# Loading the weights of a bilinear form as float32 from SyncE instead of casting them to bf16 on the way, and multiplying in four column groups

## The chip, the cores and the metric

One core of one Trainium2 chip (trn2). The metric is device time in microseconds of that core, the median of several executions; lower is better. The time is some 1.8 us above the span of the profile, which runs from the first to the last instruction. "Fast" here means within 1.5% of the fastest run of the same kernel; ratios use fast runs.

## The reference

```python
# x: [32, 256], y: [32, 256], weight: [128, 256, 256], all float32
def reference(x, y, weight):
    return np.einsum('bi,bj,kij->bk', x, y, weight).astype(np.float32)
```

The weights are 33.55 MB and are used once; everything else is small. PE contracts over i (x against the rows of the weights), VectorE multiplies by y and sums over j.

## The kernel before

```python
    x2_sb = consts.tile([B, 2, I], f32)          # x twice, for two row groups
    nc.sync.dma_start(out=x2_sb[:, 0, :], in_=x)
    nc.sync.dma_start(out=x2_sb[:, 1, :], in_=x)
    y_sb = consts.tile([B, J], f32)
    nc.sync.dma_start(out=y_sb, in_=y)
    # ... (identity; four transposes; xT in bf16: row kg*64 + ip holds x[b, 4*ip + ic])
    w_rearr = weight.rearrange("k (ip ic) j -> ip k (ic j)", ic=CHUNK)   # CHUNK = 4: runs of 4 KiB

    for kt in range(NUM_K_TILES):                # 32 tiles of 4 k
        k0 = kt * K_TILE
        wtile = wpool.tile([P, K_HALF, CHUNK * J], bf16)                 # wpool: 4 buffers
        for kg in range(2):
            nc.gpsimd.dma_start(                 # float32 in memory, bf16 in SBUF: a cast on the way
                out=wtile[kg * HALF_P:(kg + 1) * HALF_P, :, :],
                in_=w_rearr[:, k0 + kg:k0 + K_TILE:2, :],
            )
        for ks in range(0, K_HALF, K_SUB):
            # ... (two PSUM tiles)
            for ic in range(CHUNK):
                for kg in range(2):
                    p0 = kg * HALF_P
                    nc.tensor.matmul(            # 64 rows, 32 columns, 256 moving columns
                        out=psums[kg][:B, :].rearrange("b (k j) -> b k j", k=K_SUB),
                        lhsT=xT[p0:p0 + HALF_P, ic, :],
                        rhs=wtile[p0:p0 + HALF_P, ks:ks + K_SUB, ic * J:(ic + 1) * J],
                        start=(ic == 0), stop=(ic == CHUNK - 1),
                    )
            for kg in range(2):
                # ... (per k: tensor_tensor_reduce of psum * y_sb into out_sb[:, k], 32 partitions)
    nc.sync.dma_start(out=out, in_=out_sb)
```

Of the kernel before, what the change touches and what calls it, by code (L numbers as in the profile page):

```python
# [1 line left out]

# [5 lines left out]


@with_exitstack
def kernel(
    ctx: ExitStack,
    tc: tile.TileContext,
    x: bass.AP,
    y: bass.AP,
    weight: bass.AP,
    out: bass.AP,
):
    nc = tc.nc  # L20
    P = 128

    B, I = x.shape
    _, J = y.shape
    K, _, _ = weight.shape
    assert x.shape == (B, I)
    assert y.shape == (B, J)
    assert weight.shape == (K, I, J)
    assert out.shape == (B, K)

    CHUNK = 4
    HALF_P = P // 2
    assert I == HALF_P * CHUNK
    assert K <= P
    assert K % 2 == 0

    K_TILE = 4
    assert K % K_TILE == 0 and K_TILE % 2 == 0
    K_HALF = K_TILE // 2
    NUM_K_TILES = K // K_TILE  # L40
    K_SUB = max(1, min(K_HALF, 256 // J))
    assert K_HALF % K_SUB == 0

    f32 = mybir.dt.float32
    bf16 = mybir.dt.bfloat16

    consts = ctx.enter_context(tc.tile_pool(name="consts", bufs=1))
    wpool = ctx.enter_context(tc.tile_pool(name="wpool", bufs=4))
    psum_pool = ctx.enter_context(tc.tile_pool(name="psum", bufs=4, space=bass.MemoryType.PSUM))
    tmps = ctx.enter_context(tc.tile_pool(name="tmps", bufs=2))  # L50

    x2_sb = consts.tile([B, 2, I], f32)
    nc.sync.dma_start(out=x2_sb[:, 0, :], in_=x)
    nc.sync.dma_start(out=x2_sb[:, 1, :], in_=x)
    x2_flat = x2_sb.rearrange("b two i -> b (two i)")

    y_sb = consts.tile([B, J], f32)
    nc.sync.dma_start(out=y_sb, in_=y)

    identB = consts.tile([B, B], f32)  # L60
    make_identity(nc, identB)

    xT = consts.tile([P, CHUNK, B], bf16)
    for ic in range(CHUNK):
        xt_psum = psum_pool.tile([P, B], f32)
        nc.tensor.transpose(  # L66
            out=xt_psum,
            in_=x2_flat[:, ic::CHUNK],
            identity=identB,
        )  # L70
        nc.vector.tensor_copy(out=xT[:, ic, :], in_=xt_psum)  # L71

    out_sb = consts.tile([B, K], f32)

    w_rearr = weight.rearrange("k (ip ic) j -> ip k (ic j)", ic=CHUNK)

    for kt in range(NUM_K_TILES):
        k0 = kt * K_TILE

        wtile = wpool.tile([P, K_HALF, CHUNK * J], bf16)  # L80
        for kg in range(2):
            nc.gpsimd.dma_start(  # L82
                out=wtile[kg * HALF_P:(kg + 1) * HALF_P, :, :],
                in_=w_rearr[:, k0 + kg:k0 + K_TILE:2, :],
            )

        for ks in range(0, K_HALF, K_SUB):
            psums = []
            for kg in range(2):
                psum = psum_pool.tile([P, K_SUB * J], f32)  # L90
                psums.append(psum)
            for ic in range(CHUNK):
                for kg in range(2):
                    p0 = kg * HALF_P
                    nc.tensor.matmul(  # L95
                        out=psums[kg][:B, :].rearrange(
                            "b (k j) -> b k j", k=K_SUB
                        ),
                        lhsT=xT[p0:p0 + HALF_P, ic, :],
                        rhs=wtile[p0:p0 + HALF_P, ks:ks + K_SUB,  # L100
                                  ic * J:(ic + 1) * J],
                        start=(ic == 0),
                        stop=(ic == CHUNK - 1),
                    )

            for kg in range(2):
                psum_view = psums[kg][:B, :].rearrange(
                    "b (k j) -> b k j", k=K_SUB
                )
                for kk in range(K_SUB):  # L110
                    kdst = k0 + 2 * (ks + kk) + kg
                    tmp = tmps.tile([B, J], f32)
                    nc.vector.tensor_tensor_reduce(  # L113
                        out=tmp,
                        in0=psum_view[:, kk, :],
                        in1=y_sb,
                        scale=1.0,
                        scalar=0.0,
                        op0=mybir.AluOpType.mult,
                        op1=mybir.AluOpType.add,  # L120
                        accum_out=out_sb[:, kdst:kdst + 1],
                    )

    nc.sync.dma_start(out=out, in_=out_sb)


# [1 line left out]
_INS = ['x', 'y', 'weight']  # L128
_OUTS = [((32, 128), 'float32')]


# [23 lines left out]
```

## Time and profile before

| | kernel before |
|---|---|
| time, median of 2 runs | 92.69 us (92.67 to 92.71) |
| span of the profile | 90.9 us |
| weights read, rate in the steady part | 33.55 MB, 420 GB/s (210 GB/s landed as bf16) |
| first and last weight packet | 2.81 and 85.76 us after the span's start |
| from the last weight packet to the end | 5.15 us |
| PE, VectorE, GpSimd busy | 73.9, 49.8, 38.0 us |

The lines themselves are in the prediction below. The table is read from the stream outwards: what comes before its first packet (2.81 us), its length (82.95 us), and what follows its last (5.15 us) sum to the span. The packet times are records of the trace. The view of stretches of time shows engines, clock and rate for ten microseconds in the steady part; its columns are named in the first line of the fence:

```profile
core 0: us, PE busy (x) PEld busy (x) DVE busy (x) POOL busy (x), PEclk, DMA share, GB/s
20.00:30.00 10.00, 8.89 (x62) 5.07 (x60) 5.47 (x30) 4.22 (x8) 1.00 1.12 210
```

The last number is the one to follow through this document. It counts bytes that land; for a cast from float32 to bf16 the bytes read are twice that (33.65 MB read, 16.78 landed, by the page).

### The profile page before, as it was taken

How to read it: one execution, taken by the hardware profiler on the slowest of the kernel's cores; microseconds unless marked ns; L12 is line 12 of the kernel's file. 1: busy time of each engine (PE TensorE's matmuls, PEld its weight loads, DVE VectorE, ACT ScalarE, POOL GpSimd, SP SyncE). 2: the span in 40 equal slices, each digit the busy share in tenths (PEclk: the TensorE clock that was granted, in tenths of full speed). 3: DMA queues.
4: the chain of work that ended last, by engine and by line, in shares of the span. 5: the costliest groups of instructions: out<-in, count | busy, mean ns of one | idle time of the engine just before them, and what ended most of it. 6: DMA issues, size and time to landing. Idle time of an engine off the chain costs nothing.

```text
span 90.9 us, 1569 instructions
## 1 busy us (share of the span) xinstructions
PE 73.9 (81%) x516; PEld 42.3 (47%) x516; DVE 49.8 (55%) x260; POOL 38.0 (42%) x70
## 2 busy tenths in 40 slices
PE   0248989899898989669898989898998989899970
PEld 0216444555454545435554545454555545454530
DVE  0213555676535666664556656666555565566650
POOL 5970555544435543650455554434345555500000
PEclk9999999999999999985555555555555555555555
DMA  0799999999999999999999999999999999999300
GB/s 18 121 190 186 197 208 210 207 211 213 207 208 210 208 210 209 209 209 209 211 208 212 209 209 209 211 208 215 203 210 208 211 208 212 207 210 214 53 0 7
DMA packets 9416, 16.99 MB, mean 187 GB/s; under 512 B 1088, under 2 KB 1216, under 8 KB 9408
## 3 DMA queue, kind: packets, MB, share of 16 engines
q0 software_dynamic: 9216, 16.78, 100.1%
q1 hardware_dynamic: 192, 0.11, 0.5%
q8 instruction: 4, 0.07, 0.3%
q14 instruction: 4, 0.03, 0.1%
HBM read 33.65 MB, written 0.02 MB: 370 GB/s over the span
## 4 chain that ended last, share of the span: by engine, by line
DMA 64%; PE 20%; POOL 6%; issue 6%; DVE 1%; DVEq 0%; POOLq 0%
DMA wtile<-in_weight_dram 64%; PE psum L95 20%; POOL wtile L82 6%; DVE tmp L113 1%; DVE out_sb L113 0%; POOL identB masks.py:199 0%; DVEq L150 0%; POOL identB masks.py:197 0%; POOLq masks.py:199 0%; POOLq L139 0%
## 5 line engine op out<-in xcount | busy, mean ns | idle before, releaser
L95 PE MATMUL psum<-wtile,xT 64*32 64x256 bf16 x512 | 73.2, 405 | 11.1 <-DMA wtile<-in_weight_dram 9.3
L113 DVE CUSTOM_DVE_ANT_0 tmp<-psum,y_sb 32x256 f32<-32x256 f32 x128 | 48.6, 409 | 35.4 <-PE psum L95 35.2
L95 PEld LDWEIGHTS <-xT 64*32 64x32 bf16 x512 | 41.8, 122 | 42.2 <-DMA wtile<-in_weight_dram 23.9
L82 POOL DMA_DIRECT2D wtile<-in_weight_dram x64 | 37.5, 596 | 40.7 <-PE psum L95 40.1
L113 DVE DVE_READ_ACCUMULATOR2_ANT out_sb<- 32x1 f32 x128 | 9.1, 71 | 0.0
L66 PE MATMUL xt_psum<-identB,x_sb 32*128 32x32 f32 x4 | 0.7, 300 | 3.0 <-DMA x_sb<-in_x_dram 3.0
L71 DVE CAST xT<-xt_psum 128x32 bf16<-128x32 f32 x4 | 0.6, 192 | 3.4 <-PE xt_psum L66 3.4
L66 PEld LDWEIGHTS xt_psum<-identB,x_sb 32*128 32x128 f32 x4 | 0.6, 208 | 3.0 <-POOL identB masks.py:199 3.0
masks.py:199 POOL TENSOR_SCALAR_AFFINE_SELECT identB<-identB 32x32 f32<-32x32 f32 x1 | 0.2, 229 | 0.1
masks.py:197 POOL MEMSET identB<- 32x32 f32 x1 | 0.1, 114 | 0.3 <-POOLq L139 0.3
L139 POOL MEMSET const-float32-0.0<- 128x1 f32 x1 | 0.1, 103 | 0.2 <-issue 0.2
L139 POOL MEMSET const-bfloat16-1.0<- 128x1 bf16 x1 | 0.1, 106 | 0.0
L139 POOL MEMSET const-uint8-127<- 128x1 uint8 x1 | 0.1, 106 | 0.0
L139 POOL MEMSET const-float32-1.0<- 128x1 f32 x1 | 0.1, 103 | 0.0
## 6 DMA issues: line engine op xcount, KB each, us to landing
wtile<-in_weight_dram POOLq DMA_DIRECT2D x64, 256.0 KB, 7.2
x_sb<-in_x_dram SPq DMA_DIRECT2D x2, 32.0 KB, 1.7
y_sb<-in_y_dram SPq DMA_DIRECT2D x1, 32.0 KB, 3.2
out_dram<-out_sb SPq DMA_DIRECT2D x1, 16.0 KB, 1.4
```

The costliest lines, as they stand in the source:

```text
L66: nc.tensor.transpose(out=xt_psum, in_=x2_flat[:, ic::CHUNK], identity=identB,)
L71: nc.vector.tensor_copy(out=xT[:, ic, :], in_=xt_psum)
L82: nc.gpsimd.dma_start(out=wtile[kg * HALF_P:(kg + 1) * HALF_P, :, :], in_=w_rearr[:, k0 + kg:k0 + K_TILE:2, :],)
L95: nc.tensor.matmul(out=psums[kg][:B, :].rearrange("b (k j) -> b k j", k=K_SUB), lhsT=xT[p0:p0 + HALF_P, ic, :], rhs=wtile[p0:p0 + HALF_P, ...
L113: nc.vector.tensor_tensor_reduce(out=tmp, in0=psum_view[:, kk, :], in1=y_sb, scale=1.0, scalar=0.0, op0=mybir.AluOpType.mult, op1=mybir.Al ...
L139: nc = _bacc.Bacc("TRN2", target_bir_lowering=False, num_devices=1)
```

## The change

The intent: weight loads issued by SyncE (`q1 hardware_dynamic`) instead of GpSimd (`q0 software_dynamic` on the page before), no cast, float32 products. Float32 products take longer. To pay for them, the four k of a tile go into the four column groups of PE, 32 columns each, so that one PSUM tile holds four results on 128 partitions and one reduction serves four k. The contraction has 128 rows now, two per partition, so a run of memory that goes to one partition is 2 KiB; before, four rows per partition made 4 KiB.

```diff
-    wpool = ctx.enter_context(tc.tile_pool(name="wpool", bufs=4))
+    wpool = ctx.enter_context(tc.tile_pool(name="wpool", bufs=16))
...
+    w_v = weight.rearrange("(t g) (p ic) j -> g p t (ic j)", t=T, ic=IC)     # T = 4, IC = 2: runs of 2 KiB
+    x_sb = consts.tile([B, I], f32)
+    nc.scalar.dma_start(out=x_sb, in_=x)
+    y4 = consts.tile([P, J], f32)
+    for t in range(T):
+        nc.scalar.dma_start(out=y4[t * B:(t + 1) * B, :], in_=y)
... (identity; two transposes; xT stays float32)
+    acc = consts.tile([P, G], f32)
+    for g in range(G):                                                       # G = 32
+        wt = wpool.tile([P, T, IC, J], f32)
+        pieces = [(0, T)] if g < G - 1 else [(0, 2), (2, 3), (3, 4)]
+        for lo, hi in pieces:
+            nc.sync.dma_start(
+                out=wt[:, lo:hi, :, :].rearrange("p t ic j -> p t (ic j)"),
+                in_=w_v[g][:, lo:hi, :],
+            )
+        ps = pso.tile([P, J], f32)
+        for ic in range(IC):
+            for t in range(T):
+                nc.tensor.matmul(
+                    out=ps[t * B:(t + 1) * B, :],
+                    lhsT=xT[:, ic, :],
+                    rhs=wt[:, t, ic, :],
+                    start=(ic == 0), stop=(ic == IC - 1),
+                )
+        tmp = tmps.tile([P, J], f32)
+        nc.vector.tensor_tensor_reduce(
+            out=tmp, in0=ps, in1=y4, scale=1.0, scalar=0.0,
+            op0=mult, op1=add, accum_out=acc[:, g:g + 1],
         )
... (all of the loop of the kernel before goes)
-    nc.sync.dma_start(out=out, in_=out_sb)
+    for t in range(T):
+        eng = nc.sync if t % 2 == 0 else nc.scalar
+        eng.dma_start(out=out[:, t * G:(t + 1) * G], in_=acc[t * B:(t + 1) * B, :])
```

More of the change, by code (lines that the diff above doesn't have):

```diff
@@ L21 @@
     P = 128
+    f32 = mybir.dt.float32
+    mult = mybir.AluOpType.mult
+    add = mybir.AluOpType.add
     B, I = x.shape
@@ L25 @@
     K, _, _ = weight.shape
-    assert x.shape == (B, I)
-    assert y.shape == (B, J)
-    assert weight.shape == (K, I, J)
-    assert out.shape == (B, K)
-    CHUNK = 4
-    HALF_P = P // 2
-    assert I == HALF_P * CHUNK
-    assert K <= P
-    assert K % 2 == 0
-    K_TILE = 4
-    assert K % K_TILE == 0 and K_TILE % 2 == 0
-    K_HALF = K_TILE // 2
-    NUM_K_TILES = K // K_TILE
-    K_SUB = max(1, min(K_HALF, 256 // J))
-    assert K_HALF % K_SUB == 0
-    f32 = mybir.dt.float32
-    bf16 = mybir.dt.bfloat16
+    T = P // B
@@ L47 @@
+    IC = I // P
+    G = K // T
+    assert T * B == P and IC * P == I and G * T == K
     consts = ctx.enter_context(tc.tile_pool(name="consts", bufs=1))
-    wpool = ctx.enter_context(tc.tile_pool(name="wpool", bufs=4))
-    psum_pool = ctx.enter_context(tc.tile_pool(name="psum", bufs=4, space=bass.MemoryType.PSUM))
+    wpool = ctx.enter_context(tc.tile_pool(name="wpool", bufs=16))
+    psx = ctx.enter_context(tc.tile_pool(name="psx", bufs=1, space=bass.MemoryType.PSUM))
+    pso = ctx.enter_context(tc.tile_pool(name="pso", bufs=6, space=bass.MemoryType.PSUM))
@@ L50 @@
     tmps = ctx.enter_context(tc.tile_pool(name="tmps", bufs=2))
-    x2_sb = consts.tile([B, 2, I], f32)
-    nc.sync.dma_start(out=x2_sb[:, 0, :], in_=x)
-    nc.sync.dma_start(out=x2_sb[:, 1, :], in_=x)
-    x2_flat = x2_sb.rearrange("b two i -> b (two i)")
-    y_sb = consts.tile([B, J], f32)
-    nc.sync.dma_start(out=y_sb, in_=y)
-    identB = consts.tile([B, B], f32)
-    make_identity(nc, identB)
-    xT = consts.tile([P, CHUNK, B], bf16)
-    for ic in range(CHUNK):
-        xt_psum = psum_pool.tile([P, B], f32)
-        nc.tensor.transpose(
-            out=xt_psum,
-            in_=x2_flat[:, ic::CHUNK],
-            identity=identB,
-        )
-        nc.vector.tensor_copy(out=xT[:, ic, :], in_=xt_psum)
@@ L73 @@
-    out_sb = consts.tile([B, K], f32)
-    w_rearr = weight.rearrange("k (ip ic) j -> ip k (ic j)", ic=CHUNK)
-    for kt in range(NUM_K_TILES):
-        k0 = kt * K_TILE
-        wtile = wpool.tile([P, K_HALF, CHUNK * J], bf16)
-        for kg in range(2):
-            nc.gpsimd.dma_start(
-                out=wtile[kg * HALF_P:(kg + 1) * HALF_P, :, :],
-                in_=w_rearr[:, k0 + kg:k0 + K_TILE:2, :],
-            )
-        for ks in range(0, K_HALF, K_SUB):
-            psums = []
-            for kg in range(2):
-                psum = psum_pool.tile([P, K_SUB * J], f32)
-                psums.append(psum)
-            for ic in range(CHUNK):
-                for kg in range(2):
-                    p0 = kg * HALF_P
-                    nc.tensor.matmul(
-                        out=psums[kg][:B, :].rearrange(
-                            "b (k j) -> b k j", k=K_SUB
-                        ),
-                        lhsT=xT[p0:p0 + HALF_P, ic, :],
-                        rhs=wtile[p0:p0 + HALF_P, ks:ks + K_SUB,
-                                  ic * J:(ic + 1) * J],
-                        start=(ic == 0),
-                        stop=(ic == CHUNK - 1),
-                    )
-            for kg in range(2):
-                psum_view = psums[kg][:B, :].rearrange(
-                    "b (k j) -> b k j", k=K_SUB
-                )
-                for kk in range(K_SUB):
-                    kdst = k0 + 2 * (ks + kk) + kg
-                    tmp = tmps.tile([B, J], f32)
-                    nc.vector.tensor_tensor_reduce(
-                        out=tmp,
-                        in0=psum_view[:, kk, :],
-                        in1=y_sb,
-                        scale=1.0,
-                        scalar=0.0,
-                        op0=mybir.AluOpType.mult,
-                        op1=mybir.AluOpType.add,
-                        accum_out=out_sb[:, kdst:kdst + 1],
-                    )
@@ L124 @@
-    nc.sync.dma_start(out=out, in_=out_sb)
+    w_v = weight.rearrange("(t g) (p ic) j -> g p t (ic j)", t=T, ic=IC)
[4 more added lines that the diff above has]
+        nc.scalar.dma_start(out=y4[t * B:(t + 1) * B, :], in_=y)
+    ident = consts.tile([B, B], f32)
+    make_identity(nc, ident)
+    xt_ps = psx.tile([P, IC, B], f32)
+    for ic in range(IC):
+        nc.tensor.transpose(out=xt_ps[:, ic, :], in_=x_sb[:, ic::IC], identity=ident)
@@ new lines @@
+    xT = consts.tile([P, IC, B], f32)
+    nc.vector.tensor_copy(out=xT, in_=xt_ps)
+    acc = consts.tile([P, G], f32)
[8 more added lines that the diff above has]
+        ps = pso.tile([P, J], f32)
+        for ic in range(IC):
+            for t in range(T):
[9 more added lines that the diff above has]
+            op0=mult, op1=add, accum_out=acc[:, g:g + 1],
+        )
```

## The prediction

The rate of 27.2 GB/s per engine stands, because two records of the trace give it: 8 KiB took 307 ns and 1 KiB 44 ns, so 7168 bytes more took 263 ns more, 27.25 GB/s. The sum came to 92.7 + 2.5 - 1.8 + 0.5 = 93.9 us. One term in it has lost a part: of the tail's 5.2 to 6 us (+0.5), about 2 us for the last five products are cut. The half clock is read from the lengths of records: where the trace of the kernel before has clock records, products last 269 ns at 1.0 (36.9 to 40.3 us) and 417 ns at 0.5 (from 40.3 us to the end).

> **What bounds the kernel now.** I read the page from the end backwards: the chain of work that ended last, then the row of slices, then the queues, then the groups of instructions.
>
> ```profile
> DMA  0799999999999999999999999999999999999300
> GB/s 18 121 190 186 197 208 210 207 211 213 207 208 210 208 210 209 209 209 209 211 208 212 209 209 209 211 208 215 203 210 208 211 208 212 207 210 214 53 0 7
> ...
> q0 software_dynamic: 9216, 16.78, 100.1%
> ...
> HBM read 33.65 MB, written 0.02 MB: 370 GB/s over the span
> ## 4 chain that ended last, share of the span: by engine, by line
> DMA 64%; PE 20%; POOL 6%; issue 6%; DVE 1%; DVEq 0%; POOLq 0%
> ```
>
> The last line, the chain, is mostly waiting for weights (64%). The DMA row is full from slice 2 to slice 36. GB/s counts what lands: 210, because float32 is cast to bf16 on the way, so about 420 are read (33.65 MB read, 16.78 landed). The queue's packets add up to 100% of the span of 16 engines although the stream doesn't fill the span, so packets overlap a little: the bound is the 16 DMA engines, not the issuing.
>
> ```profile
> L95 PE MATMUL psum<-wtile,xT 64*32 64x256 bf16 x512 | 73.2, 405 | 11.1 <-DMA wtile<-in_weight_dram 9.3
> L113 DVE CUSTOM_DVE_ANT_0 tmp<-psum,y_sb 32x256 f32<-32x256 f32 x128 | 48.6, 409 | 35.4 <-PE psum L95 35.2
> L82 POOL DMA_DIRECT2D wtile<-in_weight_dram x64 | 37.5, 596 | 40.7 <-PE psum L95 40.1
> ...
> wtile<-in_weight_dram POOLq DMA_DIRECT2D x64, 256.0 KB, 7.2
> ```
>
> GpSimd waits 40.1 us for buffers, yet that is harmless: a load lands 7.2 us after issue, and 512 KiB read at 420 GB/s take 1.25 us, so about six loads are always queued. PE at 73.2 us busy looks near its limit, but its records overlap. The timeline of PE at 33 to 35 us shows weight loads in pairs starting at 33.47, 33.66, 33.87, 34.08 and 34.30 us: a pair of products (two row groups, 64 rows each) every 0.21 us, so 16 products of a tile take 8 x 0.21 = 1.7 us plus about 0.4 of latency, of the 2.5 us in which the tile arrives.
>
> The packet records of the trace give the pace. Weight packets (4 KiB read, 2 KiB written) run from 2.8 to 85.8 us after the span's start; in the steady part 512 of them take 5.07 us over 16 engines, 158 ns per packet and engine, 414 GB/s read. After the last packet 5.1 us remain until 90.9: the last products (to 88.0), the last reduction (88.6), and about 2.3 us to write the output. The measured time, 92.69, is 1.8 above the span.
>
> [...]
> - [...]the shortest 8 KiB packet took 307 ns (301 at 27.2 GB/s), the shortest 1 KiB packet of the x load 44 ns (37.6), so a packet costs its bytes over 27.2 GB/s plus about 6.3 ns. For the 4 KiB reads that says 157 ns; 158 was seen.
> - [...]
> - [...]No float32 product other than a transpose is in this trace.
> - [...]The trace shows the half clock most of the way ([...]records of 417 ns) with some 269 ns records between 30 and 43 us. It shows two row groups together; column groups it doesn't show.
>
> **The change part by part.**
>
> 1. *Bytes over the DMA engines.* HBM reads stay at 33.55 MB. The written bytes double to 33.55 MB, but the engines were paced by the reads, so this costs nothing unless the write side adds its own limit. What does change is the size of a run: 2 KiB instead of 4 KiB read per packet, hence 16,384 packets instead of 8,192, each with the 6.3 ns again. A packet: 2048 / 27.2 = 75.3 ns, plus 5 to 6.3 = 80.3 to 81.6 ns (estimate from the records above). Per engine 1,024 packets: 82.2 to 83.6 us, and 34 completion writes of 9 to 22 ns, 0.3 to 0.7 us. Sum about 83.4, against 512 x 158 = 80.9 before: **+2.5 us**. If queued packets overlap so well that the fixed part vanishes, it is 77 to 80.
>
> 2. *Start.* The first weight load leaves SyncE first thing (about 0.75 us, where the x load is now) instead of GpSimd at 1.29, and x, y go on ScalarE. The x packets started 1.0 us after their issue, so the weights start near 1.8 rather than 2.8: **-1.0**. GpSimd's 4.1 us of issuing its first seven loads made the ramp slow (121 GB/s in slice 1, 190 in slice 2); the first 512 packets took 6.15 us instead of 5.07. With big loads issued by SyncE I take off **-0.8**.
>
> 3. *GpSimd.* Its 64 issues, 37.5 us, go. They were beside the stream, so nothing more is gained. SyncE issues 34 loads; one of 32 rows takes 0.33 to 0.41 us now. A load of 512 runs may take longer, but it has 2.6 us, and 16 buffers let the first half of the weights be issued without any wait.
>
> 4. *PE.* 512 bf16 products become 256 in float32, each over all 128 rows, 32 columns of the array, 256 moving columns. [...]A tile of 1 MiB has 8 of them and arrives every 32 x 81 ns, about 2.6 us. [...]so PE stays hidden.
>
> 5. *VectorE.* 128 reductions become 32, over 128 partitions with the same 256 elements each, so by the same 409 ns: from 48.6 + 9.1 to about 12.2 + 2.3 us. Hidden before and after, apart from the last.
>
> 6. *Tail.* Now: 5.1 us after the last packet. Afterwards the last 256 KiB piece holds back the first-half product of its k, and because the inner loop runs over k, all four second-half products behind it: five float32 products[...]. Reduction 0.7 with its semaphores; output by two stores on each of two queues, 2.3 + 0.3. With 0.3 for landing, 5.2 to 6: **+0.5**.
>
> Sum: 92.7 + 2.5 - 1.8 + 0.5 = 93.9. With the fixed part of packets hidden (3 to 5 us less) it would be 89 to 91. I put the middle, weighted to the first, at **92.8**.
>
> **The rivals.**
> - *Still DMA-bound, slightly slower or equal* (my main line). For it: the packet records fit one formula from 1 to 8 KiB. Against: nothing shows 2 KiB packets queued back to back on a hardware queue. Time 92 to 95.
> - *DMA-bound and faster.* For it: recorded packets of weights last 172 ns at a pitch of 158, so some overlap exists[...]. Time 87 to 91.
> - *PE becomes the bound.* For it: [...]no sign in this trace that column groups run together. [...]Against: two row groups do overlap here[...]. I give it one chance in six.
> - *SyncE's issuing or the buffer wait becomes the bound.* Sixteen buffers are 42 us of stream ahead; it would need an issue of over 2.6 us. Little chance.
>
> **Range and chances.** The DMA-bound cases centre on 92.8 with a spread of some 2.5; 2% is 1.9 us, that is 90.8 to 94.5. About half of the weight lies within, a quarter below (hidden packet costs, shorter start), and a quarter above, of which more than half is PE-bound. Range 88.5 to 97.5; the PE rival's long tail lies beyond it.
>
> **What would show it.** Stream pace: the GB/s row at about 400 (25 per engine); 410 or more means that the fixed cost of a packet is hidden, under 390 that writing float32 or the hardware queue costs more than I thought. Start: GB/s already in slice 1 near its full value, first landing of a 1 MiB load before 5 us. PE: idle time before products put down to DMA, in nearly every tile; if instead SyncE waits for PE and the DMA row has holes in the second half, PE was the bound. [...]Tail: from the last landing to the end some 5.5 us. What would make me most wrong is float32 products that don't overlap over column groups[...].

## The result, and the profile after

| | before | after |
|---|---|---|
| time, median | 92.69 us | 99.80 us (99.78 to 99.81, 2 runs) |
| span | 90.9 us | 97.9 us |
| first and last weight packet | 2.81, 85.76 us | 1.87, 92.14 us |
| length of the stream | 82.95 us | 90.27 us |
| last packet to end | 5.15 us | 5.81 us |
| rate of reading, steady | 420 GB/s | 387 GB/s |

The ratio is 1.078 (95% interval 1.071 to 1.085): slower, and outside the predicted range. A ratio here is the mean time of one kernel's fast runs over that of the other's fast runs of the same rounds, so it isn't quite the ratio of the medians quoted.

From the page of the changed kernel, the rows and groups that answer to those of before:

```profile
DMA  2999999999999999999999999999999999998100
GB/s 28 289 376 359 386 386 387 388 387 388 388 381 387 388 387 387 388 386 388 388 383 388 386 387 387 388 384 386 384 387 386 388 388 388 386 387 323 49 0 7
...
q1 hardware_dynamic: 17024, 33.56, 94.0%
...
HBM read 33.72 MB, written 0.02 MB: 344 GB/s over the span
...
DMA 66%; SPq 18%; PE 10%; issue 1%; ACTq 0%; DVE 0%; DVEq 0%
...
L69 PE MATMUL ps<-wt,xT 128*32 128x256 f32 x512 | 62.4, 632 | 27.4 <-DMA wt<-in_weight_dram 27.4
...
L76 DVE CUSTOM_DVE_ANT_0 tmp<-ps,y 128x256 f32<-128x256 f32 x32 | 13.6, 425 | 76.2 <-PE ps L69 71.6
...
wt<-in_weight_dram SPq DMA_DIRECT2D x31, 1024.0 KB, 14.4
```

The DMA row is full from slice 1 to slice 35 (the first slice is slice 0), PE waits 27.4 us for weights in nearly every tile, VectorE is busy for 13.6 us: the kernel is still bound by its loads, and the loads are slower. They land at 387 GB/s, where 420 were read before. A load of 1 MiB lands 14.4 us after its issue, and at 387 GB/s a MiB takes 2.7 us, so some five loads are always queued. The 18% of SyncE's queue in the chain are issues that take 2.5 us each; I took that for a wait for room in the queue, which was a guess (e7 below tests whether it is a limit).

The timeline of PE and VectorE around one tile (start, duration, engine, line, operation, number of records):

```profile
41.37 0.23 PEld L69 LDWEIGHTS ps<-wt,xT 128*32 128x32 f32 x8 [1.62 <-DVE acc L76]
41.40 1.93 PE L69 MATMUL ps<-wt,xT 128*32 128x256 f32 x16 [0.77 <-DMA wt<-in_weight_dram]
...
43.39 0.43 DVE L76 CUSTOM_DVE_ANT_0 tmp<-ps,y 128x256 f32<-128x256 f32 x1 [2.27 <-PE ps L69]
```

A tile has 8 products and 16 records, so a record is half a product. Its 16 records are done in 1.93 us, and the bracket says that PE had stood idle for 0.77 us before them, waiting for weights: PE has room. Why 1.93 us also means that four groups ran together is worked out with experiment e8.

So most of the time lost is in one place: 0.94 us gained before the stream, 0.66 lost after it, and 7.32 lost in it; together 7.04 of span.

### The profile page after: what moved, and what is told of

Same layout as the page of the kernel before. It is cut to its first block, busy times and chain, and to the rows that moved or that the text cites. A ratio compares the mean times of both kernels' runs of the same rounds, so it can differ in the third digit from the quotient of the medians.

```text
span 97.9 us, 1265 instructions
## 1 busy us (share of the span) xinstructions
PE 62.8 (64%) x514; PEld 22.3 (23%) x514; DVE 14.1 (14%) x65; POOL 0.5 (1%) x6
## 3 DMA queue, kind: packets, MB, share of 16 engines
q1 hardware_dynamic: 17024, 33.56, 94.0%
## 4 chain that ended last, share of the span: by engine, by line
DMA 66%; SPq 18%; PE 10%; issue 1%; ACTq 0%; DVE 0%; DVEq 0%
DMA wt<-in_weight_dram 60%; SPq L62 18%; PE ps L69 10%; DMA y<-in_y_dram 6%; ACTq L43 0%; DVE tmp L76 0%; DVEq L109 0%
## 5 line engine op out<-in xcount | busy, mean ns | idle before, releaser
L69 PE MATMUL ps<-wt,xT 128*32 128x256 f32 x512 | 62.4, 632 | 27.4 <-DMA wt<-in_weight_dram 27.4
L69 PEld LDWEIGHTS ps<-wt,xT 128*32 128x32 f32 x512 | 22.0, 158 | 67.1 <-DVE acc L76 39.1
L76 DVE CUSTOM_DVE_ANT_0 tmp<-ps,y 128x256 f32<-128x256 f32 x32 | 13.6, 425 | 76.2 <-PE ps L69 71.6
L76 DVE DVE_READ_ACCUMULATOR2_ANT acc<- 128x1 f32 x32 | 2.7, 83 | 0.0
## 6 DMA issues: line engine op xcount, KB each, us to landing
wt<-in_weight_dram SPq DMA_DIRECT2D x31, 1024.0 KB, 14.4
```

The source lines that it names most:

```text
L69: nc.tensor.matmul(out=ps[t * B:(t + 1) * B, :], lhsT=xT[:, ic, :], rhs=wt[:, t, ic, :], start=(ic == 0), stop=(ic == IC - 1),)
L76: nc.vector.tensor_tensor_reduce(out=tmp, in0=ps, in1=y4, scale=1.0, scalar=0.0, op0=mult, op1=add, accum_out=acc[:, g:g + 1],)
```

## The experiments

Eighteen kernels were run, in five groups, each beside runs of the kernel before on the same chip. The pitch is the time that one DMA engine takes per 2 KiB of float32 read, 16 x 2048 bytes over the rate of reading between 20 and 30 us (387 GB/s give 84.7 ns). The run length is what goes from memory to one partition without a break; the offset is where the weight buffers start in SBUF, in bytes beyond a multiple of 256, as the compiled program places them.

| | queue, lands as | run | offset | GB/s read | pitch, ns | time, us | ratio to before |
|---|---|---|---|---|---|---|---|
| before | GpSimd, bf16 | 4 KiB | 0 | 420 | 78.0 | 92.69 | |
| after | SyncE, float32 | 2 KiB | 128 | 387 | 84.7 | 99.80 | 1.078 |
| e1 | SyncE, float32 | 4 KiB | 128 | 408 | 80.3 | 94.29 | 1.017 |
| e2 | SyncE, float32 | 8 KiB | 128 | 420 | 78.0 | 92.23 | 0.992 |
| e3, k of a tile adjacent | SyncE, float32 | 2 KiB | 128 | 387 | 84.7 | 99.28 | 1.070 |
| e4 | GpSimd, float32 | 2 KiB | 128 | 387 | 84.7 | 100.74 | 1.086 |
| e5 | GpSimd, float32 | 4 KiB | 128 | 408 | 80.3 | 95.53 | 1.027 |
| e6 | GpSimd, bf16 | 2 KiB | 0 | 412 | 79.5 | 93.86 | 1.009 |
| e7 | SyncE and ScalarE | 2 KiB | 128 | 387 | 84.7 | 98.82 | 1.063 |
| e8, one column group | SyncE, float32 | 2 KiB | 0 | 407 | 80.5 | 125.89 | 1.352 |
| e9, loads alone | SyncE, float32 | 2 KiB | 128 | 387 | 84.7 | 98.17 | 1.060 |
| e10, loads alone | SyncE, float32 | 8 KiB | 128 | 421 | 77.8 | 90.92 | 0.981 |
| e11, no reductions | SyncE, float32 | 2 KiB | 128 | 387 | 84.7 | 99.12 | 1.070 |
| e12, one product a tile | SyncE, float32 | 2 KiB | 128 | 387 | 84.7 | 98.72 | 1.067 |
| e13 | SyncE, float32 | 2 KiB | 0 | 409 | 80.1 | 94.39 | 1.017 |
| e14 | SyncE, float32 | 2 KiB | 224 | 387 | 84.7 | 99.63 | 1.074 |
| e15 | SyncE, float32 | 2 KiB | 32 | 387 | 84.7 | 99.24 | 1.069 |
| e16, kernel before, shifted | GpSimd, bf16 | 4 KiB | 128 | 420 | 78.0 | 92.79 | 1.003 |
| b1 | SyncE, float32 | 4 KiB | 0 | 420 | 78.0 | 92.46 | 0.996 |
| b2 | SyncE, float32 | 8 and 2 KiB | 0 | 428 | 76.6 | 98.73 | 1.062 |

### First group: the run, the place in memory, the queue (e1 to e4)

My theory after the result was that a run has a fixed cost, larger than I had taken it to be, and that shorter runs pay it more often (A). Rivals: writing float32 costs (B), the hardware queue is slow (C), the four k of a tile, 8 MiB apart, hinder each other in memory (D).

**e1**, 4 KiB runs with everything else the same. The edit reads the wrong rows (two 4 KiB runs per partition instead of four of 2 KiB); the result is wrong.

```diff
-    w_v = weight.rearrange("(t g) (p ic) j -> g p t (ic j)", t=T, ic=IC)
+    w_v = weight.rearrange("(h g kp) (ip ic) j -> g (kp ip) h (ic j)", h=2, kp=2, ic=4)
...
+            wf = wt.rearrange("p (h t) ic j -> p h (t ic j)", h=2)      # the load fills wf[:, h, :]
```

> The changed kernel with its weights read in 4 KiB runs (two per partition and tile) instead of 2 KiB (four), same queue, same bytes, same products; the result is wrong on purpose. Theory A (each packet has a fixed cost beside its bytes, and the run length is the cause): 2 KiB packets had a pitch of 85 ns per engine; with 75 ns for 2 KiB more, 4 KiB packets have a pitch of about 160 ns, 512 of them 82 us instead of 87, so the time falls by about 5, to 94.5 us, and the GB/s row shows about 410. Theory B (writing float32 costs, since twice the bytes land): the GB/s row stays near 387 and the time near 99.8. Theory C (the hardware queue is slow in itself): also unchanged.

**e2**, one 8 KiB run per partition; wrong result.

```diff
+    w_v = weight.rearrange("(g kp) (ip ic) j -> g (kp ip) (ic j)", kp=4, ic=8)
...
+            wf = wt.rearrange("p t ic j -> p (t ic j)")
+            nc.sync.dma_start(out=wf[:, lo * 512:hi * 512], in_=w_v[g][:, lo * 512:hi * 512])
```

> The same with one 8 KiB run per partition and tile; wrong result on purpose. Theory A: pitch 85 + 3 x 75 = 310 ns, 256 packets per engine, 79.5 us, so about 7.5 us under the changed kernel, near 92.3, GB/s about 422. Theories B and C: unchanged near 99.8.

Measured: 94.29 and 92.23 us. The stretch from 20 to 30 us of the changed kernel, of e1 and of e2, one line from each:

```profile
20.00:30.00 10.00, 5.96 (x52) 1.97 (x48) 1.73 (x8) 0.00 (x0) 1.00 1.05 387
```

```profile
20.00:30.00 10.00, 6.69 (x64) 2.37 (x64) 1.33 (x7) 0.00 (x0) 0.66 1.02 408
```

```profile
20.00:30.00 10.00, 5.74 (x60) 1.87 (x49) 1.40 (x7) 0.00 (x0) 0.70 1.01 420
```

The rate rises with the run, 387, 408, 420, at the same bytes landed; B and C, as far as they said that the rate can't rise, are out. A run takes 84.7, 160.6 and 312.1 ns, which is 9 ns plus the bytes at 27.0 GB/s per engine. A fixed cost of 9 ns, where I had used 5 to 6.3, would explain the changed kernel's pitch. It looked settled, and it wasn't: these three kernels share something that the fit can't see.

**e3**, the four k of a tile next to each other in memory (columns of the result permuted), and **e4**, the loads issued by GpSimd:

```diff
-    w_v = weight.rearrange("(t g) (p ic) j -> g p t (ic j)", t=T, ic=IC)
+    w_v = weight.rearrange("(g t) (p ic) j -> g p t (ic j)", t=T, ic=IC)     # e3
...
-            nc.sync.dma_start(
+            nc.gpsimd.dma_start(                                            # e4
```

> The changed kernel with the four k of a tile next to each other in memory (256 KiB apart instead of 8 MiB), 2 KiB runs as before; the columns of the result are permuted on purpose. Theory D (the four streams 8 MiB apart hinder each other in memory): GB/s rises from 387 to over 400 and the time falls by 3 us or more, to under 97. Theory A: no change, 99.8 within 0.5.

> The changed kernel with the weight loads issued by GpSimd instead of SyncE, everything else the same, result right. Theory C (the hardware queue is slower than GpSimd's): the pitch falls from 85 towards 80 ns, the time by 4 us or more, to under 96. Theory A: the pitch stays at 85 within 1 ns; the time stays at 99.8 or rises by about 1 for the later start.

Measured: 99.28 and 100.74 us, both at 387 GB/s. D and C fall. e4's page has one more thing:

```profile
q0 software_dynamic: 8736, 33.56, 90.5%
```

These are half as many packets as on SyncE's queue (17,024), and the records give 4,096 bytes each: GpSimd's queue put two runs into one packet, and the rate stayed where it was. What costs doesn't go with the number of packets.

### Second group: float32 or bf16, two queues, one column group (e5 to e8)

**e5** is e1 issued by GpSimd (wrong result); **e6** is the changed kernel with GpSimd's cast to bf16 and bf16 products, still 2 KiB read per run (right result); **e7** puts the loads on SyncE and ScalarE in turn.

```diff
-        wt = wpool.tile([P, T, IC, J], f32)
+        wt = wpool.tile([P, T, IC, J], bf16)          # e6, and xT in bf16, loads by nc.gpsimd
...
-            nc.sync.dma_start(
+            (nc.sync if g % 2 == 0 else nc.scalar).dma_start(     # e7
```

> Float32 weights in 4 KiB runs, issued by GpSimd (the 4 KiB variant with the other queue); wrong result on purpose. The 2, 4 and 8 KiB runs on SyncE fit 9.0 ns per run plus the bytes at 27.06 GB/s per engine: 84.7, 160.4, 311.7 ns. The kernel before, 4 KiB runs from GpSimd with a cast, shows about 156. Theory F (the 4 ns between them come from writing float32 instead of bf16): this run shows 160 ns, 409 GB/s, and 95.3 us, the 94.3 of the SyncE variant plus 1 for the later start. Theory Q (they come from the hardware queue): 156 ns, 419 GB/s, and about 93.3 us.

> The changed kernel with its 2 KiB runs, but loaded by GpSimd with the cast to bf16, and bf16 products; result right within bf16. Theory A (the length of the run that is read sets the cost): about 85 ns per run, the GB/s row at about 193 landed, and 99.5 to 101 us, although this kernel has the cast and the queue of the kernel before. Theory F (writing float32 is what costs): about 78 ns, 209 landed, and 93 us. A value between, near 82 to 83 ns and 98 us, would say that both count, most for the run.

> The changed kernel with its weight loads put on SyncE and ScalarE in turn. Theory I (SyncE's issuing, which takes 2.5 us a load, paces the stream, or one queue can't hide the fixed cost of a run): faster by 2 us or more. Theory A (the 16 engines are the limit, SyncE's issue time is only a wait for room in the queue): 99.8 within 0.7, GB/s 387, each issue about twice as long.

e5 took 95.53 us at 408 GB/s: at 4 KiB as at 2 KiB the queue doesn't matter, apart from a start about 1 us later. e7 took 98.82 us at 387 GB/s: SyncE's issuing is not a limit. The issues were expected to become twice as long and became shorter instead (medians of 1.2 us on SyncE and 1.6 on ScalarE), so what the 2.5 us wait for is not shown. e6 was a miss for theory A. With the same 2 KiB runs it lands 206 GB/s, so it reads 412:

```profile
20.00:30.00 10.00, 2.47 (x32) 0.55 (x31) 1.73 (x8) 2.96 (x4) 1.00 1.24 206
```

That is 79.5 ns a run against 84.7, and 93.86 us. Short runs alone, then, cost little; short runs that land as float32 cost much. Or so it seemed.

**e8** was meant for the PE rival of the prediction: all products in the first column group, reductions on 32 partitions, right result.

```diff
-        ps = pso.tile([P, J], f32)
-        for ic in range(IC):
-            for t in range(T):
+        ps = pso.tile([B, T, J], f32)
+        for t in range(T):
+            for ic in range(IC):
                 nc.tensor.matmul(
-                    out=ps[t * B:(t + 1) * B, :],
+                    out=ps[:, t, :],
...
+    acc = consts.tile([B, T, G], f32)                 # was [P, G]; four reductions a tile on 32 partitions
```

> The changed kernel with all float32 products in the first column group, one after the other, and the reductions on 32 partitions; result right. If the four groups are what keeps the products hidden, PE becomes the bound: [...]with PE near 100% busy[...]. If PE had room anyway, 99.8 stays.

Measured: 125.89 us, with PE at the limit. The group of its products, and the stretch from 20 to 30 us:

```profile
L69 PE MATMUL ps<-wt,xT 128*32 128x256 f32 x512 | 113.1, 385 | 1.9 <-DMA wt<-in_weight_dram 1.9
```

```profile
20.00:30.00 10.00, 10.00 (x48) 5.08 (x47) 4.36 (x24) 0.00 (x0) 1.00 1.05 407
```

Two readings. First, one by one a record takes 113.1 us / 512 = 221 ns, at a granted clock that the view gives as 1.00. In the changed kernel a record lasts 632 ns instead of 385, the mark of the half clock: the trace of e13 (below) holds both clocks, and the median record lasts 379 ns where the granted clock is 1.0 and 634 where it is 0.5. The changed kernel's clock row reads 9 throughout because its trace has no clock record before 95.0 us. One by one, 16 records take 16 x 221 ns, 3.5 us, at the full clock; at the half clock it would be about twice that, 7.1 us (an estimate: in the kernel before, pairs of products start 0.11 us apart where the granted clock is 1.0 and 0.21 us apart where it is 0.5). They took 1.93. They also start in fours, between 41.40 and 41.42, 41.80 and 41.85, 42.23 and 42.27, 42.65 and 42.70 us. So all four column groups do run together, on float32, and are worth 26 us against the changed kernel.

Second, what nobody had asked for: the loads of e8, 2 KiB float32 runs from SyncE like those of the changed kernel, ran at 407 GB/s. This contradicts theory A in its first form outright, and "float32 costs" with it.

### Third group: do the products hinder the loads? (e9 to e12)

The visible difference of e8 was its products and reductions, so the next theory was that four groups reading float32 at once, or VectorE on 128 partitions, hinder the writes into SBUF. **e9** keeps the loads of the changed kernel but products and reduction only for the last tile; **e10** does the same with 8 KiB runs; **e11** drops the reductions alone; **e12** keeps one product a tile and all reductions. All four give wrong results.

```diff
+        if g < G - 1:
+            continue          # e9, e10: ahead of the products; e11: ahead of the reduction
...
+                if g > 0 and g < G - 1 and (ic > 0 or t < T - 1):
+                    continue  # e12: one product a tile, into one PSUM tile
```

> The changed kernel's loads, 2 KiB runs, with products and reduction for the last tile only; wrong result on purpose. Why: with the products in one column group the same loads ran at 407 GB/s, not 387, 80.5 ns a run. Theory S (reading float32 in four column groups, or VectorE's work beside it, hinders the loads' writes into SBUF): 407 GB/s or more, 80 ns, stream about 4.5 us shorter; time about 94 to 95. Theory A alone (a fixed 9 ns per run, whatever runs beside): 387 and about 99.

> The same with one 8 KiB run per partition and tile. With the products beside, 8 KiB runs had 420 GB/s, 311.7 ns. Theory S1 (the hindrance costs some 4.4 ns per run): 307 ns, 427 GB/s. Theory S2 (it costs per byte): 16 to 18 ns less, above 440 GB/s. If it stays at 420, the hindrance exists only where the runs are short. Time 91.5 or less.

> The changed kernel with all products but the reduction of the last tile alone; wrong result on purpose. Theory S-PE (PE's reads are what hinders): 387 GB/s and about 99.8. Theory S-DVE (VectorE's reads and writes are): 407 and about 95.

> The changed kernel with all 32 reductions on 128 partitions, but one product a tile instead of eight (all eight for the first and last tile); wrong result on purpose. Theory S-PE: 405 GB/s or more and 95 us. Theory S-DVE: 387 and about 99.5.

The theory fell at once. e9, with PE and VectorE idle:

```profile
20.00:30.00 10.00, 0.00 (x0) 0.00 (x0) 0.00 (x0) 0.00 (x0) 1.00 1.05 387
```

387 GB/s with nothing beside the loads, and in e11 and e12 too. e10 has 421, as e2 had 420 with all the products. In the steady part products and reductions cost the loads next to nothing (84.7 ns a run in e9 against 85.0, by the packet records between 20 and 80 us). (The whole stream of e9 is 1.5 us shorter than that of the changed kernel, 88.81 against 90.27 us, nearly all of it in the first and last twentieth of the weights.)

### Fourth group: where the buffers start (e13 to e15)

Something else had to separate e8 and e6 from the others. Both change the size of a small tile that lies ahead of the weight buffers: e8's accumulator takes 512 bytes per partition instead of 128, e6's xT 128 instead of 256. In the changed kernel the compiled program puts the first weight buffer at byte 19072 of each partition, 128 beyond a multiple of 256; in e8 at 19456, in e6 at 18944, in the kernel before at 20480, all multiples of 256. e1 to e5, e7 and e9 to e12 share the 19072, which is why no comparison among them could show it. **e13** moves the buffers (and what else lies behind the accumulator) by 128 bytes and does nothing else; **e14** and **e15** move them to other offsets. All results are right.

```diff
-    acc = consts.tile([P, G], f32)
+    acc_wide = consts.tile([P, G + 32], f32)    # e13: 19200, offset 0; e14: G + 24, offset 224; e15: G + 40, offset 32
+    acc = acc_wide[:, 0:G]
```

> The changed kernel with one edit: the accumulator is 128 bytes per partition wider, so that the weight buffers behind it start at a multiple of 256 bytes (19200) instead of 128 beyond one (19072). Result right. Why: of all runs so far with 2 KiB float32 runs, the one at 407 GB/s (products in one column group) is the one whose buffers happened to start at a multiple of 256; loads alone, without products, stayed at 387. Theory L (a run that doesn't start at a multiple of 256 bytes in SBUF costs more): 407 GB/s, 80.5 ns, and 4.5 us less, 95.3 us, with all products in four groups. Theory P (the single column group, its clock or its waits were the cause): 387 and 99.8.

The expectations of e14 and e15 also held a theory L1, by which the cost grows with the offset. L2 is a cost that is the same at every offset; P is that of e13.

> The same with 96 bytes of padding: the buffers start 224 bytes beyond a multiple of 256. [...]Theory L2 ([...]whatever the offset): as with 128 bytes, 387 GB/s and 99.8. Theory P: 99.8.

> The same with 160 bytes of padding: 32 beyond a multiple of 256. [...]Theory L2: 387 GB/s and 99.8. Theory P: 99.8.

The same stretch of e13, e14 and e15 in this order:

```profile
20.00:30.00 10.00, 5.57 (x64) 2.24 (x64) 1.37 (x8) 0.00 (x0) 0.84 1.05 409
```

```profile
20.00:30.00 10.00, 6.80 (x60) 2.42 (x60) 1.73 (x8) 0.00 (x0) 1.00 1.05 387
```

```profile
20.00:30.00 10.00, 6.80 (x63) 2.35 (x60) 1.73 (x8) 0.00 (x0) 1.00 1.04 387
```

128 bytes of padding take the changed kernel from 99.80 to 94.39 us (ratio to before 1.017, interval 1.014 to 1.021) with every product still in four groups. Offsets of 32, 128 and 224 cost the same: 4.6 ns a run by these rates, 4.4 to 4.5 by the packet records between 20 and 80 us (85.0 and 85.1 against 80.6), the latter including the completion writes (packets of 4 bytes, 9 to 14 ns each in the changed kernel). The multiple that counts is 256: 19072 is a multiple of 128 and is slow, 19200 is no multiple of 512 and is fast. 1,024 runs per engine x 4.4 ns = 4.5 us of stream, and the span shrinks by 4.8 (97.9 to 93.1).

How a start off the multiple costs this is not shown. A cost that grew with the offset would, scaled from the 4.4 ns at 128 bytes, be 1.1 ns at 32 and 7.7 ns at 224 (an estimate from e13 and the changed kernel); the three cost the same, so it does not grow so. Whether it is paid on the side of the write is not shown either; shown is the effect of the start, its size, and that it is the same at three offsets.

### Fifth group: the other kernel, and two attempts to beat both (e16, b1, b2)

**e16** shifts the buffers of the kernel before by 128 bytes in the same way.

```diff
-    out_sb = consts.tile([B, K], f32)
+    out_wide = consts.tile([B, K + 32], f32)
+    out_sb = out_wide[:, 0:K]
```

> The kernel before with 128 bytes of padding ahead of its weight buffers, so that they too start 128 beyond a multiple of 256 bytes (20608; before, 20480). It reads 4 KiB and writes 2 KiB of bf16 per run. If the offset adds a fixed 4.4 ns to every run's write and that is on the path, 512 runs per engine are 2.3 us: 95.0 us. If the write of a cast run, half as many bytes as its read, is hidden behind the read, nothing changes: 92.7 within 0.5 and 210 GB/s landed.

Measured: 92.79 us, ratio 1.003 (0.9995 to 1.007), and the rate unchanged:

```profile
20.00:30.00 10.00, 8.84 (x61) 5.04 (x58) 5.29 (x27) 3.78 (x7) 1.00 1.12 210
```

So at this offset the kernel before pays nothing: the start of the buffers is a cost that the change brought onto the path. The queue is not what spares it, since e4 and e5 use the same queue and are as slow as on SyncE (387 and 408 GB/s). The cast reads 4 KiB and writes 2 KiB per run, and that the shorter write stays hidden behind the read is only a guess: no run separates the length of the write from the cast.

**b1** puts the findings together: float32 by SyncE in 4 KiB runs at offset 0, 64 rows a product, eight k at once (two row groups by four column groups), the last tile loaded by parts of the contraction. Right result. For the 110 us of the expectation: in e8 the products, one by one, kept PE busy for 113.1 us.

```diff
+    w_v = weight.rearrange("(t g kp) (ip ic) j -> g (kp ip) t (ic j)", t=T, kp=2, ic=4)
+    acc_wide = consts.tile([P, 2 * G + 32], f32)      # offset 0
...
+        for ic in range(IC):
+            for t in range(T):
+                for kp in range(2):
+                    nc.tensor.matmul(
+                        out=pss[kp][t * B:(t + 1) * B, 0:J],
+                        lhsT=xT[kp * H:(kp + 1) * H, ic, :],
+                        rhs=wt[kp * H:(kp + 1) * H, t, ic * J:(ic + 1) * J],
```

> A version that should beat both: float32 weights by SyncE in 4 KiB runs, buffers at a multiple of 256 bytes, 64 rows a product in two row groups and four column groups (eight k at once), the last tile loaded by quarters of the contraction. Result right. If L and the run length are the causes: 4 KiB aligned have a pitch of 156 ns, 419 GB/s, stream about 82 us from 1.9 us on, tail 5: 90 to 91 us. If the eight products don't overlap, PE becomes the bound and it takes 110 us or more.

Measured: 92.46 us, ratio 0.996 (0.992 to 1.0007). The rate is as expected (156.0 ns for a 4 KiB run where e1, off the multiple, took 160.6; the 4.6 ns are again those of one run, though it is twice as long),

```profile
20.00:30.00 10.00, 7.02 (x128) 3.06 (x128) 1.55 (x8) 0.00 (x0) 0.66 1.03 420
```

but the ends are not: the last products start at 86.1 us, as in the kernel before, because the stream takes longer to reach its rate (by bytes landed its first twentieth takes 1.9 us more than a steady one; before, 1.2) and to end (1.3 us more in the last twentieth; before, 0.9; its last MiB goes in runs of 1 KiB). It equals the kernel before, with float32 products, and is not shown to beat it.

**b2** loads 112 of the k in 8 KiB runs (32 rows a product, four row groups by two column groups at a time, 16 k a step) and the last 16 k like e13; right result. Its edit is a rewrite of the loop after the pattern of b1. The passes of its expectation are records of products: in b1 56 of them took 1.93 us, 34 ns each.

> A second version that should beat both: 112 of the 128 k in float32 with 8 KiB runs by SyncE (32 rows a product, four row groups, up to eight products at a time), the last 16 k in 2 KiB runs with small last pieces, all buffers at a multiple of 256 bytes. Result right. 8 KiB runs had 311.7 ns at the bad offset; less 4.4 they are 307: 896 runs of 2 KiB worth at 76.8 and 128 at 80.5 are 79.1 us, from 1.8 on with a ramp of some 2 to 83, tail 5, and 1.8: 90.0 us. If PE's 64 passes a MiB (34 ns each in the 4 KiB version, 2.2 us of the 2.45 in which it lands) don't keep up, 95 or more.

Measured: 98.73 us, ratio 1.062 over the fast runs (two of its six executions, and the profiled one, count as slow, so only coarse readings are taken from its profile). The stream reaches 428 GB/s between 20 and 30 us, but PE is now the bound; who waited for whom:

```profile
PEld ps L87 <- issue: 26.3, 53, 3.2
PE ps L87 <- issue: 14.0, 9, 2.7
```

```profile
q8 instruction: 14, 0.23, 0.9%
```

In the second line PE stood 14.0 us, in nine pieces of up to 2.7 us, with "issue" named, which means that it waited for nothing that the view shows, and not for weights. The last line, from the list of DMA queues on the page, shows something else that moves: 14 loads of instructions, 16 KiB each, where the changed kernel has 4. This kernel has 1,792 records of products of 32 rows where the changed kernel has 512 records in all. By the trace every one of the nine pieces ends 2.2 to 2.4 us after such a load starts. That PE waits for its next instructions there is a guess from one slow execution; no run tests it. The granted clock adds to it: in three stretches of 6.8 us it is 0.5. The prediction's rival of PE as the bound exists, only not in the kernel it was named for.

## Why the prediction was wrong, point by point

- **The bound** (DMA engines before and after): right. e9 has no work beside the loads and is only 1.6 us faster than the changed kernel (98.17 against 99.80).
- **Start, "-1.0"**: right, first packet at 1.87 instead of 2.81 us.
- **Bytes over the DMA engines, "A packet: 2048 / 27.2 = 75.3 ns, plus 5 to 6.3 = 80.3 to 81.6 ns"**: this is the step that failed. The changed kernel takes 84.7 to 85.0 ns. The formula is right for buffers that start at a multiple of 256 bytes: e13 takes 80.1 to 80.6. It lacked a term of 4.4 ns per run for float32 buffers that don't, which 1,024 runs make 4.5 us of the 7.3 us that the stream lost. The prediction said that the doubled write "costs nothing unless the write side adds its own limit" and didn't look at where the write lands. Nor did its own records show the term: its weight packets all had the cast, and its 8 KiB packets are loads of instructions (queue 14). It also named a sign, under 390 GB/s, and two causes for it, writing float32 or the hardware queue; the sign came (387), and e13 (409 with float32 from SyncE) and e4 (387 from GpSimd) rule out both. The run length, which it did count at +2.5 us, is worth about 1,024 x 80.6 - 512 x 157.4 = 1.9 us by the packet records of e13 and of before.
- **Ramp, "-0.8"**: wrong in sign, small. The first twentieth of the weights took 1.0 us longer than a steady twentieth before and 1.5 us after; the GB/s row starts sooner but dips in slice 3 (359), and the first MiB landed at about 6.8 us, where "before 5 us" was expected. The last twentieth, which the prediction didn't count, took 0.9 us longer than a steady one before and 1.6 after.
- **SyncE's issuing**: hidden, as predicted (e7), though an issue takes 2.5 us.
- **PE**: right that it stays hidden; it waits 27.4 us for weights. The four groups run together at the half clock, 16 records in 1.93 us; one by one, the case that the forecast feared, costs 125.9 us (e8). The clock could not be read from the clock row; the lengths of the records show it.
- **VectorE**: right, 32 reductions of 425 ns where 409 were assumed.
- **Tail, "+0.5"**: 0.66. The last products ended 2.4 us after the last packet (92.14 to 94.53 us).
- **The sum**: the prediction's own sum was 93.9 us, and e13, the changed kernel with the missing term taken away, takes 94.4. The step from 93.9 down to 92.8, made for overlap that might hide a run's fixed cost, was the wrong way: in e13 that cost shows in full. That the sum comes so close to e13 is in part luck: for e13 the ramp was counted about 1.2 us too low and the run length 0.6 too high.

## What to carry to other kernels

Before blaming the length of runs, the queue or the cast for a slow load, look at where the buffer starts in SBUF: a small tile ahead of it can shift it off a multiple of 256 bytes, and each run of a float32 load then paid 4.4 ns here (a load with a cast to bf16 paid nothing). Padding the small tile is free to try, and was worth 5.4 us of 99.8 here. And when several experiments agree on a neat fit, ask what they all share; the fit of 9 ns per run was exact and half of it was an accident of layout.
